# Fourier weight tiles read tile by tile, q swaps issued at the eviction, value products one score block later: a two-layer encoder on one core

## The chip, the cores and the metric

The kernel runs on one core of a Trainium2 chip. The metric is the device time of one execution in microseconds (us); lower is better. Before the change it took 2400.25 us, the median of three runs (2400.01 to 2401.22). All other times here are us too, from the span's start where they name a moment.

## The reference, cut to what matters

A trunk of two layers over 272 tokens (16 meta tokens and 256 others), 2048 channels, float32:

```python
h = rmsnorm(x)
q, k, v, f, ga, gf = split(h @ w_in)
q, k = rope_2d(rmsnorm(q)), rope_2d(rmsnorm(k))      # 8 query heads, 2 key heads, 128 wide
a = attention(q, k, v) @ w_attn_br                   # meta tokens, then two blocks of 128 queries
fr = real(fft2(f, axes=(tokens, 128 channels)))      # 8 channel groups
s = fr @ w_four
x = x + (sigmoid(ga) * a + sigmoid(gf) * s) @ w_out
h = rmsnorm(x)
x = x + (silu(conv3(h @ w_up_gate)) * (h @ w_up_val)) @ w_down
```

The output is x without the meta tokens.

## The kernel before

**Precision and weight tiles.** Every matrix product is made from float32 operands that are split into a high and a low part; three matmuls (high by high, high by low, low by high) stand for one. A weight tile is 128 partitions by 1024 (four blocks of 128 rows by 256 columns, 512 KB). Its way is: a DMA on SyncE's queue into a `raw` buffer (`load_raw`, L264; seven buffers), a cast on ScalarE to the high part `wh` (L300), a subtraction on VectorE to the low part `wl` (L303). `wh` and `wl` have three buffers each. The tiles come in one list in the order in which the matmul groups use them (`order`, then `chunks`).

**Groups.** `group` (L346) makes two output tiles of 128 rows in PSUM from several weight tiles. PSUM has eight tiles, four with the tag "mm" for these groups and four with the tag "aux" for everything else. A group that asks for a "mm" tile gets the one that was given out longest ago, and its first matmul into it waits until the last eviction from it is done.

**Fourier groups.** `four_group` (L388) multiplies the Fourier features by `w_four`, two weight tiles a group, eight groups a layer. By symmetry each output half m (0 and 1) takes two PSUM tiles, an even and an odd sum (`ps_s00`, `ps_s01` for m=0, `ps_s10`, `ps_s11` for m=1), and has 17 matmuls: 8 on the first weight tile, 8 on the second (L407 on `wh`, L408 on `wl`), and one with `w64` (L413). Then `s_evac` copies the second parts of both tiles out on ScalarE (L1206), adds the first parts on VectorE (L1207, `se` and `so`: these are the last reads of the two PSUM tiles) and multiplies the result with the gate. In layer 0 the two weight tiles of a Fourier group are folded first: VectorE makes sums and differences of two raw halves into `wpm` (L291, two instructions, one buffer), and `wh` and `wl` are made from that. In layer 1 they come folded from memory.

**What orders the work.** `advance` queues splits of coming weight tiles (`LOOK` = 2 tiles ahead) and starts loads; `pump` emits one queued split, or all up to a tile; `step` advances one of the generators in `shadow`, which emit the small work of normalisation, rotation and attention between the matmuls. This gives a program order; a scheduler then sets the order on each engine, and each engine runs its own in order. `tc.manual_schedule` (around q1 of layer 1) keeps the written order on the engines that it names.

**q and its rotation.** Each of four q groups a layer is evicted by `head_evac` (squares on ScalarE L910, the weighted copy `qp` on VectorE L911). `q_stage` then calls `swap` (L924): four DMAs on SyncE's queue that exchange blocks of 32 partitions of `qp` into `qs`. `rope` multiplies `qs` (L928) and `qp` (L929), adds them (L930), casts (ScalarE, L931) and subtracts (L933). In layer 1, between q1 and q2, stand the matmuls of `folded_f` (L843 on `wh`, L847 on `wl`).

**Attention.** `attention` goes over nine items of a key head: one for the meta tokens and eight (head h, query block i). For each: `scores` (three matmuls, maximum, exponential), `normalise` (L1086 writes `pn`), `transposed` (three transposes, L1095, into PSUM; ScalarE copies the high parts to `PH`, L1108, VectorE the low parts to `PL`, L1109), and after both blocks of a head `values` (L1118 to L1121: products of V with PH and PL).

Of the kernel before, what the change touches and what calls it, by code (L numbers as in the profile page):

```python
# [10 lines left out]
F32 = mybir.dt.float32  # L11
# [5 lines left out]
P = 128  # L17
# [16 lines left out]
MG = 2  # L34
# [43 lines left out]
TH = T // 2 + 2  # L78
# [79 lines left out]
def al(ap):  # L158
    if len(ap.shape) == 3:
        return ap.rearrange("p r (b a) -> p r a b", b=2)  # L160
    return ap.rearrange("p (b a) -> p a b", b=2)


def st2(ap):
    if len(ap.shape) == 3:
        return ap.rearrange("p r (a b) -> p r a b", b=2)
    return ap.rearrange("p (a b) -> p a b", b=2)
# [11 lines left out]
def encoder_kernel(ctx, tc, xT, params, consts, bmat, cfold, csign, w_fl, w_f64c, w_in, w_abr, w_four, w_f64, w_out, w_up, w_down, w_vn, w_dn, w_dt, out):  # L179
    nc = tc.nc  # L180
# [73 lines left out]
    raws, splits = {}, {}  # L254
    RAW, LOOK = 7, 2
# [13 lines left out]
    def advance(upto):  # L269
        while st["raw"] < min(upto + RAW + 2 * (upto > first_mix), len(chunks)):  # L270
            load_raw(st["raw"])
            st["raw"] += 1
        while st["fetch"] < min(upto, len(chunks)):
            i = st["fetch"]
            if i in folded:
                todo.append((i, lambda i=i: fold_w(i)))
            for a in (0, 2) if i <= 3 else (0,):
                todo.append((i, lambda i=i, a=a: split_w(i, a, a + 2 if i <= 3 else CW)))
            st["fetch"] += 1

    def pump(upto=None):
        if upto is None:
            if todo:
                todo.pop(0)[1]()
        while upto is not None and todo and todo[0][0] <= upto:
            todo.pop(0)[1]()
# [101 lines left out]
    def four_group(key, fr, x64, w64, evac):  # L388
        k, chs = order[st["grp"]]
        assert k == key, (k, key)  # L390
        st["grp"] += 1
        i0 = st["next"]
        st["next"] += len(chs)
        advance(i0 + 1 + LOOK)
        pump(i0 + 1)
        ws = [splits.pop(i0 + j) for j in range(2)]
        for m in range(MG):
            sl = slice(m * P, (m + 1) * P)
            ps = [psum.tile([P, 512], F32, tag="mm", name=f"ps_s{m}{e}") for e in range(2)]
            for j in range(2):  # L400
                h, lo = ws[j]
                for c in range(2):
                    kt = 2 * j + c
                    for e in range(2):
                        x = al(fr[:, kt, e])
                        o2 = st2(ps[e][:, :2 * TH].rearrange("p (r n) -> p r n", r=2))
                        nc.tensor.matmul(o2, h[:, 2 * e + c, sl], x, start=kt == 0, stop=False)  # L407
                        nc.tensor.matmul(st2(ps[e][:, :TH]), lo[:, 2 * e + c, sl], x[:, 0], start=False, stop=e == 1 and kt == 3)  # L408
                    step()
                    pump()  # L410
                if m == 1 and j == 0:
                    advance(i0 + 2 + LOOK)
            nc.tensor.matmul(st2(ps[0][:, :TH]), w64[:, sl], al(x64), start=False, stop=True)  # L413
            evac(m, ps)

    def first_groups(pss):
        assert order[st["grp"]][0] == (0, "f01")
# [191 lines left out]
    for l in range(DEPTH):  # L609
        last = l == DEPTH - 1  # L610
        lo = 14 if last else 0
# [4 lines left out]
        with tc.tile_pool(name=f"mix{l}", bufs=1) as mp:  # L616
# [285 lines left out]
            def head_evac(ps, gcol, name, lo):  # L902
                hp = rt(name)
                sq = rt(name + "s")
                if lo:
                    nc.gpsimd.memset(hp[:, :, 0:lo], 0.0)
                    nc.gpsimd.memset(sq[:, :, 0:lo], 0.0)
                for m in range(MG):
                    x = de(ps[m][:, :T - lo])
                    nc.scalar.activation(hv(sq[:, m, lo:T]), x, AF.Square)  # L910
                    nc.vector.scalar_tensor_tensor(hv(hp[:, m, lo:T]), x, gcol, hv(rstdB[:, lo:T]), op0=ALU.mult, op1=ALU.mult)  # L911
                return hp, sq
# [8 lines left out]
            def swap(hp):  # L921
                qs = rt("qs")
                for b in range(4):
                    tc.keep_in_program_order(nc.sync.dma_start(qs[32 * b:32 * b + 32, :, :], hp[32 * (b ^ 1):32 * (b ^ 1) + 32, :, :]))  # L924
                return qs
# [82 lines left out]
            for pn in pns:  # L1008
                nc.gpsimd.memset(pn[:, 0:P], 0.0)

            def q_stage(i, qp, qsq):
                kv, j = i // 2, i % 2
                sl = slice(2 * j, 2 * j + 2)
                if j == 0:
                    qvs.append(small.tile([P, 9], F32, tag="qv", name="qv"))
                    qsms.append(small.tile([P, 2, 4, NM], F32, tag="sqm", name="sqm", bufs=2))
                qv, qsm = qvs[kv], qsms[kv]
                qs = swap(qp)
                yield 3
                nc.vector.tensor_copy(qsm[:, :, 2 * j:2 * j + 2, :], qsq[:, :, 0:NM].unsqueeze(1).to_broadcast([P, 2, 2, NM]))  # L1020
                d4 = qv[:, 4 * j:4 * j + 4]
                sums_t(d4, [qsq[:, m, a:b] for m in range(MG) for a, b in BLK[1:]])
                d4 = d4.rearrange("p (m i) -> p m i", m=2)
                nc.vector.tensor_tensor(d4, d4, bc2(tok2[:, 1:3]), op=ALU.mult)
                if j:
                    yield 1
                    sums_t(qv[:, 8:9], [qsm.rearrange("p r h t -> p (r h t)")])
                    nc.vector.tensor_tensor(qv[:, 8:9], qv[:, 8:9], tok2[:, 0:1], op=ALU.mult)
                    nc.vector.tensor_scalar(qv, qv, 1.0 / HD, EPS, op0=ALU.mult, op1=ALU.add)
                    rq = small.tile([P, 9], F32, tag="rq", name="rq")  # L1030
                    pow_half(rq, qv)
                yield 6 - j
                yield from rope(qp, qs, qH[kv][:, sl, :], qL[kv][:, sl, :])
                if j:
                    rqs.append(rq)
                    if kv == 0:
                        push(attend(), 5)
# [9 lines left out]
            def attention(kv, rq):  # L1047
# [75 lines left out]
                    nc.vector.tensor_tensor(hv(qL[kv][:, h, lo:T]), de(po[:, :W]), hv(qH[kv][:, h, lo:T].bitcast(F32)), op=ALU.subtract)  # L1123

                items = [None] + [(h, i) for h in range(4) for i in range(2)]
                prev, ready, due = None, [], []
                for item in items + ["end", "end"]:
                    cur = None
                    if item != "end":
                        pe, sm = scores(item)  # L1130
                    yield 2
                    if item != "end":
                        cur = (item, normalise(pe, sm))
                    yield 1
                    if prev is not None:
                        transposed(*prev)
                        if prev[0] is not None and prev[0][1] == 1:
                            due.append(prev[0][0])
                        yield 1
                    if ready:  # L1140
                        values(ready.pop(0))
                    if prev is not None:
                        yield 1
                    ready, due = ready + due, []
                    prev = cur
                while ready:
                    values(ready.pop(0))
                    yield 1

            qH, qL = [], []  # L1150
            for i in range(4):
                if not (last and i == 1):
                    ps = group((l, "q", i), xr(lo), W)
                    qq = head_evac(ps, prm[:, P_QN + l:P_QN + l + 1], "qp", lo)
                if last:
                    if i in (0, 2):
                        until(hold, "vt" if i == 0 else "fold")
                        for t_, n in ((qH, "q1"), (qL, "q2")):
                            t_.append(mp.tile([P, 4, T], F32R, tag=n + "ab"[i // 2], name=n))
                elif i == 0:  # L1160
                    until(hold, "vt")
                    until(hold, "fold")
                    for t_, n in ((qH, "q1"), (qL, "q2")):
                        t = mp.tile([P, NH, T], F32R, tag=n, name=n)
                        t_ += [t[:, 0:4], t[:, 4:8]]
                if last and i == 1:
                    until(hold, "ahead")
                    with tc.manual_schedule(engines={mybir.EngineType.DVE}):
                        ps = group((l, "q", i), xr(lo), W)
                        with tc.manual_schedule(engines={mybir.EngineType.Activation}):  # L1170
                            qq = head_evac(ps, prm[:, P_QN + l:P_QN + l + 1], "qp", lo)
                            folded_f(slots, E)
                    o1_tiles()
                    push(folded_chan(E), 1)
                push(q_stage(i, *qq), 1)
# [395 lines left out]
```

## Time and profile before

| | |
|---|---|
| median of 3 runs | 2400.25 us |
| the profiled execution's own time | 2399.24 us |
| its span on the core | 2397.2 us |
| mean granted TensorE clock | 0.998 |
| TensorE busy | 2367.0 us (99%) |
| VectorE busy | 1819.8 us (76%) |
| ScalarE busy | 1307.1 us (55%) |

PE is TensorE (matmuls), PEld its weight loads, DVE VectorE, ACT ScalarE, SP or SPq SyncE and its DMA queue. L12 is line 12 of the kernel before; in the kernel after, lines behind `four_group` stand one to three higher. In the rows of a timeline the first two numbers are start and duration, and a bracket at the end gives the idle time of the engine before the instruction, and what ended it; "x2" joins instructions of one kind that follow each other. Rows of waits give the total, the number, and the longest. Rows of windows give the stretch and its length, then busy time (and instructions) of the engines asked for, the granted clock, the DMA share and GB/s. An engine's instructions overlap a little (a matmul of 0.28 starts 0.11 after the one before), so a row's place is read from starts.

### The profile page before, as it was taken

How to read it: one execution, taken by the hardware profiler on the slowest of the kernel's cores; microseconds unless marked ns; L12 is line 12 of the kernel's file. 1: busy time of each engine (PE TensorE's matmuls, PEld its weight loads, DVE VectorE, ACT ScalarE, POOL GpSimd, SP SyncE). 2: the span in 40 equal slices, each digit the busy share in tenths (PEclk: the TensorE clock that was granted, in tenths of full speed). 3: DMA queues.
4: the chain of work that ended last, by engine and by line, in shares of the span. 5: the costliest groups of instructions: out<-in, count | busy, mean ns of one | idle time of the engine just before them, and what ended most of it. 6: DMA issues, size and time to landing. Idle time of an engine off the chain costs nothing.

```text
span 2397.2 us, 47622 instructions
## 1 busy us (share of the span) xinstructions
PE 2367.0 (99%) x18992; PEld 2305.8 (96%) x18992; DVE 1819.8 (76%) x2889; ACT 1307.1 (55%) x1893; POOL 133.4 (6%) x265
## 2 busy tenths in 40 slices
PE   9999999999999999999999999999999999999999
PEld 8999999999999999999998999999989999999988
DVE  7787867877767556777568887776878889888798
ACT  6555534554444334444455555445676666666565
POOL 0000100100000000000000000000000000000000
PEclk9999999999999999999999999999999999999999
DMA  7556999989999999999875646888889988988887
GB/s 278 173 159 216 289 295 304 297 278 346 313 303 327 315 330 314 316 327 308 264 256 181 190 150 216 264 291 247 290 294 301 323 291 301 305 304 279 260 279 251
DMA packets 171215, 660.69 MB, mean 276 GB/s; under 512 B 19424, under 2 KB 24672, under 8 KB 170096
## 3 DMA queue, kind: packets, MB, share of 16 engines
q1 hardware_dynamic: 152528, 538.07, 64.0%
q0 software_dynamic: 17024, 117.45, 19.4%
q8 instruction: 149, 2.44, 0.4%
q10 hardware_dynamic: 1440, 2.13, 0.3%
q14 instruction: 74, 0.61, 0.1%
HBM read 635.91 MB, written 136.31 MB: 322 GB/s over the span
## 4 chain that ended last, share of the span: by engine, by line
PE 81%; DVE 6%; ACT 2%; DMA 1%; issue 1%; SPq 0%; POOL 0%; ACTq 0%; DVEq 0%; POOLq 0%
PE ps_p L1415 9%; PE ps_ug L374 6%; PE ps_ug L373 6%; PE ps_ug L372 6%; PE ps_uv L368 4%; PE ps_d L374 3%; PE ps_uv L373 3%; PE ps_uv L372 3%; PE ps_d L373 3%; PE ps_uv L374 3%; PE ps_d L372 3%; DVE wl L303 3%; PE ps_o L372 2%; PE ps_o L373 2%; PE ps_o L374 2%; PE ps_uv L369 2%
## 5 line engine op out<-in xcount | busy, mean ns | idle before, releaser
L303 DVE TENSOR_TENSOR wl<-raw,wh 128x1024 fp32r<-128x1024 f32 (+1 forms) x937 | 1127.6, 1217 | 469.8 <-ACT wh L300 458.4
L300 ACT CAST wh<-raw 128x1024 fp32r<-128x1024 f32 (+1 forms) x937 | 964.6, 1040 | 752.1 <-PE ps_ug L373 197.2
L374 PE MATMUL ps_ug<-xHL,wl 128*128 128x272 f32 (+1 forms) x1408 | 390.6, 277 | 0.8 <-DVE wl L303 0.6
L372 PE MATMUL ps_ug<-xHL,wh 128*128 128x272 f32 (+1 forms) x1408 | 390.7, 278 | 0.0
L373 PE MATMUL ps_ug<-xHL,wh 128*128 128x272 f32 (+1 forms) x1408 | 390.0, 277 | 0.0
L373 PEld LDWEIGHTS ps_ug<-xHL,wh 128*128 128x128 f32 x1408 | 267.4, 190 | 2.1
L372 PEld LDWEIGHTS ps_ug<-xHL,wh 128*128 128x128 f32 x1408 | 267.4, 190 | 2.1
L374 PEld LDWEIGHTS ps_ug<-xHL,wl 128*128 128x128 f32 x1408 | 267.5, 190 | 1.6 <-DVE wl L303 1.5
L372 PE MATMUL ps_uv<-xHL,wh 128*128 128x272 f32 x704 | 196.4, 279 | 0.0
L373 PE MATMUL ps_uv<-xHL,wh 128*128 128x272 f32 x704 | 196.4, 279 | 0.0
L374 PE MATMUL ps_uv<-xHL,wl 128*128 128x272 f32 x704 | 196.4, 279 | 0.0
L372 PE MATMUL ps_d<-gHL,wh 128*128 128x272 f32 x704 | 196.4, 279 | 0.0
L373 PE MATMUL ps_d<-gHL,wh 128*128 128x272 f32 x704 | 196.4, 279 | 0.0
L374 PE MATMUL ps_d<-gHL,wl 128*128 128x272 f32 x704 | 196.4, 279 | 0.0
L1415 PE MATMUL ps_p<-wh,opnd 128*128 128x512 f32 x688 | 177.5, 380 | 0.5 <-ACT wh L300 0.5
L368 PE MATMUL ps_uv<-xHL,wh 128*128 128x512 f32 x448 | 150.8, 383 | 0.1
L372 PE MATMUL ps_ga<-xHL,wh 128*128 128x272 f32 (+1 forms) x512 | 144.0, 281 | 0.0
L372 PE MATMUL ps_gf<-xHL,wh 128*128 128x272 f32 (+1 forms) x512 | 143.0, 279 | 0.0
L374 PE MATMUL ps_gf<-xHL,wl 128*128 128x272 f32 (+1 forms) x512 | 141.8, 277 | 0.0
L373 PE MATMUL ps_ga<-xHL,wh 128*128 128x272 f32 (+1 forms) x512 | 141.8, 277 | 0.0
L374 PE MATMUL ps_ga<-xHL,wl 128*128 128x272 f32 (+1 forms) x512 | 141.8, 277 | 0.0
L373 PE MATMUL ps_gf<-xHL,wh 128*128 128x272 f32 (+1 forms) x512 | 141.8, 277 | 0.0
(372 smaller groups left out, 5840.8 us busy)
## 6 DMA issues: line engine op xcount, KB each, us to landing
raw<-in_w_up SPq DMA_DIRECT2D x320, 512.0 KB, 5.6
raw<-in_w_in SPq DMA_DIRECT2D x191, 512.0 KB, 4.5
raw<-in_w_down SPq DMA_DIRECT2D x88, 512.0 KB, 6.8
raw<-ft SPq DMA_DIRECT2D x80, 512.0 KB, 4.8
raw<-in_w_out SPq DMA_DIRECT2D x64, 512.0 KB, 6.5
ft<-in_w_dn POOLq DMA_DIRECT2D x30, 1024.0 KB, 12.1
raw<-in_w_dn SPq DMA_DIRECT2D x60, 512.0 KB, 5.0
raw<-in_w_abr SPq DMA_DIRECT2D x32, 512.0 KB, 5.6
```

Of the source, the lines that this page charges most:

```text
L300: nc.scalar.copy(h[:, a:b], r[:, a:b])
L303: nc.vector.tensor_tensor(lo[:, a:b], r[:, a:b], h[:, a:b].bitcast(F32), op=ALU.subtract)
L368: nc.tensor.matmul(o2, h[:, c, sl], ab, start=kt == 0, stop=False)
L369: nc.tensor.matmul(o, lo[:, c, sl], ab[:, 0], start=False, stop=kt == nk - 1)
L372: nc.tensor.matmul(o, h[:, c, sl], a, start=kt == 0, stop=False)
L373: nc.tensor.matmul(o, h[:, c, sl], b, start=False, stop=False)
L374: nc.tensor.matmul(o, lo[:, c, sl], a, start=False, stop=kt == nk - 1)
L1415: nc.tensor.matmul(st2(ps[h]), x, al(w[:, 512 * h:512 * h + 512]), start=fresh and (s_, q) in BEGIN and first, stop=(s_, q) in END and end ...
```

## The change

There are three edits.

1. `four_group` asks for all four PSUM tiles at its start and goes over the weight tiles outside: first tile for m=0 and m=1, then second tile for m=0 and m=1, each m closed by its `w64` matmul and eviction. The second tile's split need only be emitted before its half, and `advance` for the third tile comes after the first half of the group rather than after the third quarter.
2. `swap(qp)` is called right after `head_evac` and not when `q_stage` begins.
3. A head's `values` becomes ready one item later (a list `soon` between `due` and `ready`).

```diff
-        pump(i0 + 1)
-        ws = [splits.pop(i0 + j) for j in range(2)]
-        for m in range(MG):
-            sl = slice(m * P, (m + 1) * P)
-            ps = [psum.tile([P, 512], F32, tag="mm", name=f"ps_s{m}{e}") for e in range(2)]
-            for j in range(2):
-                h, lo = ws[j]
+        pss = [[psum.tile([P, 512], F32, tag="mm", name=f"ps_s{m}{e}") for e in range(2)] for m in range(MG)]
+        for j in range(2):
+            pump(i0 + j)
+            h, lo = splits.pop(i0 + j)
+            for m in range(MG):
+                sl = slice(m * P, (m + 1) * P)
+                ps = pss[m]
                 for c in range(2):
...
-                if m == 1 and j == 0:
-                    advance(i0 + 2 + LOOK)
-            nc.tensor.matmul(st2(ps[0][:, :TH]), w64[:, sl], al(x64), start=False, stop=True)
-            evac(m, ps)
+                if j:
+                    nc.tensor.matmul(st2(ps[0][:, :TH]), w64[:, sl], al(x64), start=False, stop=True)
+                    evac(m, ps)
+            if j == 0:
+                advance(i0 + 2 + LOOK)
...
-                qs = swap(qp)
...
-                    ready, due = ready + due, []
+                    ready, soon, due = ready + soon, due, []
                     prev = cur
+                ready += soon
...
                     qq = head_evac(ps, prm[:, P_QN + l:P_QN + l + 1], "qp", lo)
+                    qq += (swap(qq[0]),)
```

TensorE in layer 0's second Fourier group, before: `wh72`, `wl72` are the first weight tile's parts, `wh73`, `wl73` the second's.

```order
L407 MATMUL ps_s01_3421<-fr_122,wh72_3358 128x276
L408 MATMUL ps_s01_3421<-fr_122,wl72_3359 128x138
L407 MATMUL ps_s00_3420<-fr_122,wh73_3394 128x276
L407 MATMUL ps_s01_3421<-fr_122,wh73_3394 128x276
L407 MATMUL ps_s10_3453<-fr_122,wh72_3358 128x276
L408 MATMUL ps_s00_3420<-fr_122,wl73_3395 128x138
```

The same place after:

```order
L407 MATMUL ps_s01_3421<-fr_122,wh72_3358 128x276
L408 MATMUL ps_s01_3421<-fr_122,wl72_3359 128x138
L407 MATMUL ps_s10_3422<-fr_122,wh72_3358 128x276
L408 MATMUL ps_s10_3422<-fr_122,wl72_3359 128x138
L407 MATMUL ps_s11_3423<-fr_122,wh72_3358 128x276
```

Before, the second tile was wanted from the group's ninth matmul on; after, from the seventeenth, with `ps_s10` and `ps_s11` written in between.

VectorE around the eviction of that group's m=0, before: `wl74` and `wl75` are the third and fourth tile counted from the group's first, 72.

```order
L303 TENSOR_TENSOR wl74_3427<-raw74_3177,wh74_3426 128x1024
L1229 TENSOR_TENSOR mL_3338<-th_2123,mH_3337 128x272
L1207 TENSOR_TENSOR se_3443<-ps_s00_3420,se_3443 128x138
L1207 TENSOR_TENSOR so_3444<-ps_s01_3421,so_3444 128x138
L1209 TENSOR_TENSOR sp_3449<-se_3443,so_3444 128x138
L1210 TENSOR_TENSOR sp_3449<-se_3443,so_3444 128x134
L1212 SCALAR_TENSOR_TENSOR th_3127<-th_3127,sp_3449 128x272
L303 TENSOR_TENSOR wl75_3470<-raw75_3209,wh75_3469 128x1024
```

The same place after (L1210 is the add that was L1207):

```order
L303 TENSOR_TENSOR wl74_3429<-raw74_3158,wh74_3428 128x1024
L1232 TENSOR_TENSOR mL_3338<-th_2123,mH_3337 128x272
L303 TENSOR_TENSOR wl75_3451<-raw75_3209,wh75_3450 128x1024
L1210 TENSOR_TENSOR so_3460<-ps_s01_3421,so_3460 128x138
L1210 TENSOR_TENSOR se_3459<-ps_s00_3420,se_3459 128x138
L1212 TENSOR_TENSOR sp_3465<-se_3459,so_3460 128x138
```

The split of `wl75` (the group's first tile plus three) has moved from behind the eviction to directly ahead of its adds; on ScalarE `wh75` stands ahead of the copies in the same way. All sixteen groups show this.

SyncE's queue at layer 1's q0, before: `raw451` to `raw454` are weight loads, `qs` the swap.

```order
L264 DMA raw451_16310<-fw_66 128x1024
L264 DMA raw452_16350<-fw_66 128x1024
L264 DMA raw453_16399<-fw_66 128x1024
L924 DMA qs_16409<-qp_16385 32x2x272 x4
L264 DMA raw454_16444<-fw_66 128x1024
```

The same place after:

```order
L264 DMA raw451_16310<-fw_66 128x1024
L264 DMA raw452_16350<-fw_66 128x1024
L925 DMA qs_16393<-qp_16385 32x2x272 x4
L264 DMA raw453_16404<-fw_66 128x1024
L264 DMA raw454_16444<-fw_66 128x1024
```

The swap stands one weight load earlier.

More of the change, by code (lines that the diff above doesn't have):

```diff
@@ L1009, in encoder_kernel, with q_stage @@
                 nc.gpsimd.memset(pn[:, 0:P], 0.0)
-            def q_stage(i, qp, qsq):
+            def q_stage(i, qp, qsq, qs):
                 kv, j = i // 2, i % 2
@@ L1125, in attention @@
                 items = [None] + [(h, i) for h in range(4) for i in range(2)]
-                prev, ready, due = None, [], []
+                prev, ready, due, soon = None, [], [], []
                 for item in items + ["end", "end"]:
@@ L1171, in encoder_kernel @@
                             qq = head_evac(ps, prm[:, P_QN + l:P_QN + l + 1], "qp", lo)
+                            qq += (swap(qq[0]),)
                             folded_f(slots, E)
```

## The prediction

> **What bounds the kernel now.** I read the page first, then the waits of TensorE, then single stretches on the timeline, the chain of waits, and a table of the sixteen Fourier groups.
>
> ```profile
> PE 2367.0 (99%) x18992; PEld 2305.8 (96%) x18992; DVE 1819.8 (76%) x2889; ACT 1307.1 (55%) x1893; POOL 133.4 (6%) x265
> ```
>
> TensorE is busy 99% of the span. The change issues the same matmuls, so time can come only from TensorE's idle time, and new idle time is a loss one for one. The waits of TensorE (us in total, times, longest) name what there is to win:
>
> ```profile
> PE ps_s L408 <- DVE wl L303: 4.3, 8, 0.7
> PE ps_f L847 <- DVE wl L303: 3.9, 1, 3.9
> PE ps_pt L1095 <- DVE pn L1086: 2.9, 4, 1.3
> PE ps_pv L1119 <- DVE PL L1109: 2.2, 4, 1.2
> PE ps_pv L1118 <- ACT PH L1108: 2.0, 5, 0.5
> PE ps_s L407 <- ACT wh L300: 2.0, 5, 1.1
> ```
>
> L407/L408 are Fourier groups waiting for a weight tile (6.3), L847 is one late tile beside the q swap (3.9), L1118/L1119 the value products (4.2). Each edit aims at one of these.
>
> **Part 1, Fourier groups.** The table of windows has each group from its first matmul to the next group's first; shown are one of layer 0's first half, one of its second, layer 1's second and last, and the sum of all sixteen.
>
> ```profile
> 245.47:250.71 5.24, 4.34 (x37) 1.00 0.91 222
> 388.83:393.31 4.48, 4.12 (x36) 1.00 0.65 164
> 1473.53:1477.38 3.85, 3.85 (x36) 1.00 0.79 214
> 1668.48:1672.34 3.86, 3.86 (x36) 1.00 0.90 150
> sum 73.47, PE 66.58; mean PE 4.16
> ```
>
> Free of waits a group takes 3.86 (its 34 matmuls, two per 0.23). Layer 1's groups have nothing to win; the idle time over all sixteen, 73.47 - 66.58 = 6.9, is nearly all layer 0's.
>
> The edit spends eight matmuls (0.92) more on the first tile, so the second may come 0.9 later. But it moves two things against itself. First, half m=0 ends after three quarters of the group instead of half, 1.0 later, and the next group's first matmuls write into m=0's two PSUM tiles and wait for their VectorE adds (L1207). Second, the order of after puts the split of the weight tile three on from the group's first (wh on ScalarE, wl on VectorE; call it tile 3) ahead of those adds, where before had it behind. Layer 1, on VectorE and then ScalarE:
>
> ```profile
> 1474.79 1.22 DVE L303 TENSOR_TENSOR wl<-raw,wh 128x1024 fp32r<-128x1024 f32 x1
> 1475.92 0.76 DVE L1229 TENSOR_TENSOR mL<-th,mH 128x258 fp32r<-128x258 f32 x2
> 1476.60 0.29 DVE L1207 TENSOR_TENSOR so<-ps_s,so 128x138 f32<-128x138 f32 x1
> 1475.52 0.28 ACT L1206 COPY so<-ps_s 128x138 f32<-128x138 f32 x1 [0.19 <-PE ps_s L408]
> 1476.53 2.00 ACT L300 CAST wh<-raw 128x1024 fp32r<-128x1024 f32 x2 [0.56 <-ACT se L1206]
> ```
>
> Here the first add ends at 1476.89 and the next group starts at 1477.38: 0.49 to spare. After: tile 3 needs the buffer of the group's first tile (three buffers), which the eighth pair of matmuls leaves 1.94 after the start (8 x 0.23 and the last one's end), at 1475.47. Then wh 1.05 (half of 2.00, with its start) ends at 1476.55, wl at 1.22 ends at 1477.80, and the add 0.3 later, 1478.10: 0.72 behind 1477.38. The same chain from the group's own start holds in the other six of layer 1: 7 x 0.72 = 5.0. The first one there carries score and value work among its matmuls; I take 0.5. Layer 1: +5.5.
>
> Layer 0, first half (group at 245.47), VectorE, then the group's largest wait on TensorE:
>
> ```profile
> 246.75 1.23 DVE L303 TENSOR_TENSOR wl<-wpm,wh 128x1024 fp32r<-128x1024 f32 x1
> 248.59 1.22 DVE L303 TENSOR_TENSOR wl<-raw,wh 128x1024 fp32r<-128x1024 f32 x1
> 249.73 0.43 DVE L1229 TENSOR_TENSOR mL<-th,mH 128x272 fp32r<-128x272 f32 x1
> 250.29 0.29 DVE L1207 TENSOR_TENSOR so<-ps_s,so 128x138 f32<-128x138 f32 x1
> 248.03 0.44 PE L408 MATMUL ps_s<-fr,wl 128*128 128x138 f32 x2 [0.64 <-DVE wl L303]
> ```
>
> The second tile's low part ends at 247.98 either way; with the new order the matmuls that need it stand at 247.5, so about 0.9 of the group's 1.4 (5.24 - 3.86) goes. Nothing of it reaches the end, since VectorE works without a break from 246.75: the 1.14 of tile 3's split (start to next start) enters ahead of the adds, the second of which then ends at 250.58 + 1.14 = 251.7, the first at 251.5. The next group starts at 251.55 instead of 250.71: +0.85, three times (2.55). In the group before these, two matmuls also wait for the gate's evictions, +0.6; the first of the second half is covered, -0.1. For the last three (group at 388.83), VectorE:
>
> ```profile
> 390.26 0.43 DVE L1184 TENSOR_TENSOR th<-ps_gf,rstdB 128x272 f32<-128x272 f32 x1
> 391.76 0.30 DVE L1207 TENSOR_TENSOR so<-ps_s,so 128x138 f32<-128x138 f32 x1
> ```
>
> The fourth PSUM tile is now wanted at 389.98 but is the gate's until 390.69; the first tile's matmuls end 0.69 later at 391.4, wh at 392.45, wl at 393.6, add at 393.95 against a start at 393.31: +0.65 each, 1.95. Layer 0: 0.6 + 2.55 - 0.1 + 1.95 = +5.0. **Part 1 is +10.5.** Bounds: -6.9, if nothing waits for the adds and all tile waits go; +13, if each add also waits for ScalarE's copy behind wh (16 x 0.28 = 4.5, over half of the groups). I take +10.5, since it is put together from durations that all stand above; the likely spread is +7 to +13.
>
> The Trainium skill, "Perfetto Trace Analysis", section "Optimizing Tensor Performance", wants independent matmul groups to rotate through PSUM banks so that one's evacuation overlaps the next one's matmuls. Filling all four tiles to the end works against that; layer 1 of before, with two tiles at a time and no idle, agrees, and no run here shows the other side yet.
>
> **Part 2, the q swaps.** The chain of waits around the one late tile (start, duration):
>
> ```profile
> 1284.41 0.40 DVE qp L911
> 1286.64 0.32 SPq L264
> 1287.05 0.60 SPq L924
> 1288.98 3.83 DMA qs<-qp
> 1292.93 0.73 DVE qs L928
> 1296.45 1.23 DVE wl L303
> 1297.73 0.48 PE ps_f L847
> ```
>
> q0's eviction (L911) is done by 1284.8, but the swap's four DMAs stand on SyncE behind a weight load that waits until 1286.58 for a buffer. VectorE waits at L928 for the swap, and the low part that TensorE needs is queued behind q's rotation:
>
> ```profile
> 1288.03 2.36 DVE L303 TENSOR_TENSOR wl<-raw,wh 128x1024 fp32r<-128x1024 f32 x2
> 1292.93 0.73 DVE L928 TENSOR_TENSOR qs<-qs,cst 128x544 f32<-128x544 f32 x1 [2.54 <-DMA qs<-qp]
> ```
>
> The DMA issues in this stretch, with the us to landing at the end:
>
> ```profile
> qs<-kp SPq DMA_DIRECT2D x4, 68.0 KB, 2.4
> qs<-qp SPq DMA_DIRECT2D x4, 68.0 KB, 3.8
> ```
>
> After, only SyncE's order changes here: the swap goes ahead of that load, issues from 1284.9 to 1287.4, and lands by about 1289.8 to 1291.2 (2.4 to 3.8 after the last issue). VectorE is at work until 1290.39, so L928 starts 2.54 sooner at best and 1.7 at worst, and the low part is there at about 1295.2; TensorE's wait falls from 3.9 to about 1.4. The load passed starts 0.8 later and is not wanted for several tiles (seven raw buffers). The clock, in windows (us, TensorE busy, granted clock):
>
> ```profile
> 1293.90:1296.80 2.90, 0.00 (x0) 0.00 (x0) 2.21 (x5) 1.59 (x2) 0.00 (x0) 0.99 0.29 113
> 1296.80:1303.60 6.80, 5.87 (x27) 5.79 (x28) 4.04 (x6) 1.99 (x2) 0.00 (x0) 0.50 0.45 154
> 1303.60:1310.00 6.40, 6.40 (x59) 6.33 (x59) 6.33 (x9) 4.08 (x6) 0.00 (x0) 1.00 0.59 186
> ```
>
> 2.9 after TensorE went idle the clock fell to half for 6.8 us. The 27 matmuls there took 5.87; at the next window's 6.40/59 = 0.108 they take 2.93, so half speed cost 2.9. An idle of 1.4 ends before the point where it fell. **Part 2 is -2.5 - 2.9 = -5.4**; bounds 0 (swap lands no sooner) and -6.8 (the whole wait goes). The Trainium skill, "TensorE: Matmul & The Clock Gate", section "Part 1: The HAM clock gate", has a free-running window of 3413 ns, one of which idle halves the clock. The 6.8 us at half speed are two such, so the trace agrees; by the page too, an idle of 1.4 cannot hold a window.
>
> The other layer-1 swap that moves passes two small constant loads and later weight loads, the one in layer 0 two loads; VectorE does not wait for either in before. I cost both at nothing; 0.3 each if a weight load came late.
>
> **Part 3, value products a block later.** The largest wait is in layer 1:
>
> ```profile
> 1384.42 0.38 PE L1118 MATMUL ps_pv<-PH,VH 128*128 128x258 f32 x1 [0.51 <-ACT PH L1108]
> 1387.11 0.38 PE L1119 MATMUL ps_pv<-PL,VH 128*128 128x258 f32 x1 [1.18 <-DVE PL L1109]
> ```
>
> In layer 1 the probability tile's second half reads, by range, the block that was transposed last, whichever that is; a block later the one before it is safe, but a new one has been transposed just ahead again. So I let the outlier 1.18 shrink to 0.5 (-0.7), and two of the other seven go, at (4.2 - 0.51 - 1.18)/7 = 0.36 each (-0.7): **-1.4**. Bounds: -4.2 (all waits on PH and PL go) and +1.5 (the score blocks' own waits at L1095, 2.9, grow by half).
>
> **Sum.** 10.5 - 5.4 - 1.4 = +3.7. The profiled execution took 2399.24 (span 2397.2), 1.0 under the median of 2400.25; so the forecast is 2399.24 + 3.7 + 1.0 = **2403.9**. A measurement of this kernel can tell about 0.2% (4.8 us) from no change: "same" is 2395.45 to 2405.05.
>
> **The rivals.**
> - *The forecast*, chance 0.54, own range 2400 to 2408 (part 1 by +7 to +13): 0.02 faster, 0.42 same, 0.10 slower.
> - *The adds don't bind.* If the next group's first matmuls found their tiles free, the tile waits would go for nothing: -6.9 - 5.4 - 1.4 = -13.7, 2386.5. For: 4.48 and 5.24 stand beside 3.86. Against: the 0.49 of slack in layer 1 is smaller than the 1.0 by which m=0 ends later, even without tile 3's split. 0.14, faster.
> - *The swap gains nothing and the clock still falls* (slower). It decides if the swap lands after 1292.3: the DMA rows would need 5 us from the last issue, where 3.8 was the slowest; or if TensorE's idle still covers 1293.8 to 1296.8. Then 10.5 - 1.4 = +9.1, 2409.3. 0.18, slower.
> - *The value waits move rather than go*: with +1.5 for part 3 the sum is +6.6, 2406.8. For it: in the rows above the product waits for a block just transposed, and the order keeps such a block ahead of it. 0.14: 0.10 slower, 0.04 same.
>
> Together: faster 0.16, same 0.46, slower 0.38. The range 2395 to 2409.5 leaves out the second case and a little above the third.
>
> **What would show it.** Right: layer 1's Fourier windows at 4.5 to 4.6 with waits of matmuls L372 on L1210's adds (so/se), sixteen in all; L408 waits down to a few tenths; L847's wait near 1.4 and no window at clock 0.50. Wrong: Fourier windows at 3.86 in layer 1 (then the second case), an L847 wait over 3 (third), or waits at L1118/L1119 still above 4 in sum.

## The result, and the profile after

The changed kernel takes 2405.36 us, the median of 19 runs (2403.27 to 2407.84); the kernel before, measured beside it, 2400.36 (19 runs). The ratio is 1.0019, 95% interval [1.0012, 1.0027]: about 5 us slower (3 to 6.5 by the interval), right at the edge of the 0.2% that the prediction counts as no change. The forecast was 2403.9, with a range of 2395 to 2409.5. The profiled execution has a span of 2403.6, against 2397.2, so the two traces lie 6.4 apart.

The waits of TensorE in the kernel after (us in total, times, longest) answer to those of before:

```profile
PE ps_gf L372 <- DVE so L1210: 5.0, 5, 1.5
PE ps_a L372 <- DVE so L1210: 4.1, 8, 0.6
PE ps_ga L372 <- DVE so L1210: 2.0, 2, 1.5
PE ps_s L407 <- DVE th L1187: 1.9, 3, 0.7
PE ps_s L408 <- DVE wl L303: 1.5, 5, 0.6
PE ps_f L848 <- DVE wl L303: 1.4, 2, 1.3
PE ps_pt L1095 <- DVE pn L1086: 3.4, 5, 0.9
PE ps_pv L1119 <- DVE PL L1109: 2.1, 2, 1.1
PE ps_pv L1118 <- ACT PH L1108: 1.4, 3, 0.7
```

The first three rows are new: the groups that follow a Fourier group (gf, a, ga) wait at their first matmul for the adds `so` that evict m=0, fifteen times, 11.1 us. The sixteenth, behind layer 1's first Fourier group, does not wait for them: that group is held up inside, by a value product.

```profile
1455.29 0.38 PE L1119 MATMUL ps_pv<-PL,VH 128*128 128x258 f32 x1 [1.12 <-DVE PL L1109]
```

The fourth row is new too: `ps_s11` waits for a gate's eviction. The waits of Fourier groups for weight tiles fell from 6.3 to 1.5 (the prediction had a few tenths), the late tile's (now L848) from 3.9 to 1.3 at the longest. The value products' fell from 4.2 to 3.5, and the score blocks' (L1095) rose from 2.9 to 3.4.

The Fourier groups in windows (stretch, length, TensorE busy, clock, DMA share, GB/s), the four places shown of before, and the sum of all sixteen:

```profile
244.08:250.27 6.19, 4.50 (x36) 1.00 0.83 195
390.25:395.66 5.41, 4.23 (x36) 1.00 0.59 151
1473.16:1477.72 4.56, 4.02 (x36) 1.00 0.67 167
1672.64:1677.25 4.61, 4.03 (x37) 1.00 0.93 168
sum 84.45, PE 68.72; mean PE 4.29
```

The sum went from 73.47 to 84.45: +11.0, where the prediction had +10.5. The busy column rose by 2 as well (its ends are modelled); the number of matmuls is the same, so the length is what counts.

VectorE in layer 1's second Fourier group, then ScalarE there, after:

```profile
1476.23 1.22 DVE L303 TENSOR_TENSOR wl<-raw,wh 128x1024 fp32r<-128x1024 f32 x1
1477.37 0.30 DVE L1210 TENSOR_TENSOR so<-ps_s,so 128x138 f32<-128x138 f32 x1
1475.13 1.05 ACT L300 CAST wh<-raw 128x1024 fp32r<-128x1024 f32 x1 [0.18 <-ACT mH L1231]
1476.09 0.27 ACT L1209 COPY so<-ps_s 128x138 f32<-128x138 f32 x1
```

The group starts at 1473.16. Tile 3's cast starts 1.97 later (forecast 1.94), its low part ends at 1477.45, the add at 1477.67, and the next group starts at 1477.72. The copy was out at 1476.36, so for the 1.0 between it and the add's start the PSUM tile waits for nothing but VectorE's turn.

The late tile, and the clock behind it, after. First TensorE's row, then the windows:

```profile
1299.50 0.33 PE L848 MATMUL ps_f<-hA,wl 128*128 128x138 f32 x1 [1.26 <-DVE wl L303]
```

```profile
1298.20:1299.50 1.30, 0.04 (x2) 1.00 0.10 41
1299.50:1303.00 3.50, 3.50 (x30) 1.00 0.64 189
```

In the chain of waits there the swap now issues at 1289.27, right after the eviction, and is no wait of VectorE's any more; the clock stays at 1.00. How much that brought is read from two waits of TensorE that stand on either side in both kernels, before and then after:

```profile
1283.05 0.44 PE L918 MATMUL ps_ss<-cst,qps 128*128 128x128 f32 x2 [0.78 <-ACT qps L910]
1369.90 0.52 PE L1095 MATMUL ps_pt<-cst,pn 128*128 128x128 f32 x3 [0.62 <-DVE pn L1086]
```

```profile
1287.45 0.44 PE L919 MATMUL ps_ss<-cst,qps 128*128 128x128 f32 x2 [0.78 <-ACT qps L911]
1369.33 0.52 PE L1095 MATMUL ps_pt<-cst,pn 128*128 128x128 f32 x3 [0.60 <-DVE pn L1086]
```

The same work takes 86.85 before and 81.88 after: -4.97. The stretch between these two waits is 81.88 or 81.89 in the traces of all six kernels with the swap edit (the runs below included), and 86.48 to 86.85 in the four without it.

### The profile page after: what moved, and what is told of

It reads as the page before. It is cut to its first block, busy times and chain, and to the rows that moved or that the text cites. A ratio compares the mean times of both kernels' runs of the same rounds, so it can differ in the third digit from the quotient of the medians.

```text
span 2403.6 us, 47628 instructions
## 1 busy us (share of the span) xinstructions
PE 2366.8 (98%) x18992; PEld 2304.5 (96%) x18992; DVE 1818.9 (76%) x2889; ACT 1306.7 (54%) x1893; POOL 130.8 (5%) x265
## 4 chain that ended last, share of the span: by engine, by line
PE 85%; DVE 8%; ACT 3%; DMA 2%; issue 2%; POOL 0%; SPq 0%; DVEq 0%; ACTq 0%; POOLq 0%
PE ps_p L1418 9%; PE ps_ug L374 6%; PE ps_ug L373 6%; PE ps_ug L372 6%; DVE wl L303 4%; PE ps_uv L368 3%; PE ps_d L372 3%; PE ps_uv L374 3%; PE ps_uv L373 3%; PE ps_d L374 3%; PE ps_uv L372 3%; PE ps_d L373 3%; PE ps_o L374 2%; PE ps_o L373 2%; PE ps_o L372 2%; ACT wh L300 2%
## 5 line engine op out<-in xcount | busy, mean ns | idle before, releaser
L374 PE MATMUL ps_ug<-xHL,wl 128*128 128x272 f32 (+1 forms) x1408 | 391.0, 278 | 2.4 <-DVE wl L303 2.3
L374 PEld LDWEIGHTS ps_ug<-xHL,wl 128*128 128x128 f32 x1408 | 267.5, 190 | 3.8 <-DVE wl L303 3.5
L374 PE MATMUL ps_uv<-xHL,wl 128*128 128x272 f32 x704 | 196.4, 279 | 0.0
L374 PE MATMUL ps_d<-gHL,wl 128*128 128x272 f32 x704 | 196.4, 279 | 0.0
L372 PE MATMUL ps_gf<-xHL,wh 128*128 128x272 f32 (+1 forms) x512 | 143.3, 280 | 5.0 <-DVE so L1210 5.0
L374 PE MATMUL ps_gf<-xHL,wl 128*128 128x272 f32 (+1 forms) x512 | 141.8, 277 | 0.0
L374 PE MATMUL ps_ga<-xHL,wl 128*128 128x272 f32 (+1 forms) x512 | 141.8, 277 | 0.0
L372 PE MATMUL ps_o<-mH,wh 128*128 128x272 f32 (+1 forms) x512 | 141.8, 277 | 0.0
```

The costliest lines, as they stand in the source:

```text
L372: nc.tensor.matmul(o, h[:, c, sl], a, start=kt == 0, stop=False)
L374: nc.tensor.matmul(o, lo[:, c, sl], a, start=False, stop=kt == nk - 1)
```

## The experiments

The theory (A) is the prediction's: the Fourier loop loses some 11 us because the next group waits for the eviction of m=0's PSUM tiles; the swap wins about 5; the value products about 1. The rivals: the edits disturb each other (B), the early split on a busy VectorE costs by itself rather than through the PSUM tiles (B of the second series), m=0's later end alone makes the wait (C).

All runs are compared with the kernel before on the same chip: the first four rows on one, where it took 2400.55, the last four on another, where it took 2400.27.

| kernel | us | ratio to before, 95% interval | sixteen Fourier windows |
|---|---|---|---|
| Fourier loop alone | 2413.61 | 1.0056 [1.0042, 1.0070] | 85.2 |
| swap alone | 2396.81 | 0.9985 [0.9974, 0.9995] | |
| value products alone | 2399.82 | 0.9996 [0.9987, 1.0004] | |
| swap and values | 2395.41 | 0.9983 [0.9974, 0.9992] | 74.3 |
| after, eviction kept first | 2391.73 | 0.9971 [0.9959, 0.9982] | 71.0 |
| after, m=1 in other PSUM tiles | 2389.61 | 0.9958 [0.9946, 0.9971] | 68.3 |
| the same, values late in layer 0 only | 2388.96 | 0.9961 [0.9948, 0.9975] | 67.8 |
| Fourier loop alone, m=1 in other PSUM tiles | 2395.95 | 0.9981 [0.9972, 0.9991] | 68.1 |

**One edit at a time.** The Fourier loop alone is the new `four_group` in the kernel before.

> Only the Fourier loop (edit 1) on the kernel before. Theory A (the next group waits for the adds that evict m=0): +11 us, about 2411, the sixteen Fourier windows sum to about 84.5 as in the kernel after; the late low part at L847 and the half clock are still there. Rival B (the three edits interact, and the loss in after comes from the swap or value edits shifting the tiles): under +5, 2401 to 2405, windows under 80.

It measured +13 (interval +10 to +17), windows of 85.2: theory A for the place and the size, B is out. Here all sixteen groups are followed by a wait for the adds. The 2 beyond the expected +11 are within the interval; a half-speed stretch in the profiled execution (last section) is one possible cause.

The swap alone is the moved call:

```diff
-                qs = swap(qp)
+                    qq += (swap(qq[0]),)
```

> Only the q swap (edit 2) on the kernel before. Theory A: -5 us, about 2395: the wait at the late tile falls from 3.9 to about 1.3 (-2.6) and no window at clock 0.50 follows (-2.3 to -2.9). Rival B (the clock falls whatever the wait): -2.6, about 2397.7, with a window at clock 0.50.

-3.7 (interval -6 to -1). The time does not tell -5 from -2.6. In the trace the late tile waits 1.26 and no stretch after it shows a clock under 1.00:

```profile
1295.00 0.33 PE L847 MATMUL ps_f<-hA,wl 128*128 128x138 f32 x1 [1.26 <-DVE wl L303]
```

That is theory A for the profiled execution, which was the fastest of the eleven (2392.96). It is one of three with a mean clock of 1.000; the other eight show 0.998 or 0.999 and average 4 us more, so their clock fell somewhere; where, no trace shows.

The value products alone:

```diff
-                    ready, due = ready + due, []
+                    ready, soon, due = ready + soon, due, []
```

> Only the value products (edit 3) on the kernel before. Theory A from the trace of after: -1.5 in layer 0, +0.3 in layer 1, together -1.2, about 2399. Rival B (the waits only move): 0 +- 0.5, 2400.3. The half clock after the late tile stays in both.

-0.7, interval -3 to +1: not told from nothing. The waits of TensorE in its trace, to be read against those of before:

```profile
PE ps_f L847 <- DVE wl L303: 4.1, 1, 4.1
PE ps_pt L1095 <- DVE pn L1086: 3.4, 5, 0.8
PE ps_pv L1119 <- DVE PL L1109: 2.0, 2, 1.1
PE ps_pv L1118 <- ACT PH L1108: 1.7, 4, 0.7
```

Scores and values together wait 7.1 in both kernels (2.9 + 2.2 + 2.0, and 3.4 + 2.0 + 1.7). Of the Fourier groups, layer 0's first is 0.57 shorter than before (5.50 against 6.07) and layer 1's first 1.08 longer (7.18 against 6.10). This edit moves waits; rival B holds as well as A.

Both without the Fourier loop:

> Edits 2 and 3 without the Fourier loop. Theory A (terms add): -5.0 - 1.2 = -6.2, about 2394.2, Fourier windows at 73.5 as before. Rival B (interaction): over 2397.

-5 (interval -6 to -2): this fits terms that add, though the interval also holds rival B's 2397. The Fourier windows are back at 74.3; layer 1's first takes 7.47 of it, with a half-speed stretch that the last section shows.

**Which part of the Fourier loop loses.** Here the kernel after keeps its four PSUM tiles, but the adds stand ahead of tile 3's split:

```diff
-            nc.scalar.copy(h[:, a:b], r[:, a:b])
+            keep(i, nc.scalar.copy(h[:, a:b], r[:, a:b]))
...
+        kept.add(i0 + 3)
...
                     evac(m, ps)
-            if j == 0:
-                advance(i0 + 2 + LOOK)
+                    if m == 0:
+                        advance(i0 + 2 + LOOK)
```

`keep` holds the split of that tile in program order, on ScalarE and VectorE; the eviction's copies and adds are held in the same way. Tile 3 is also queued later, behind m=0's eviction, so the run changes the order by two means at once.

> The kernel after with its four PSUM tiles, but with the eviction of m=0 kept ahead of tile 3's split on VectorE and ScalarE (kept in program order, and the queueing of tile 3 after m=0's eviction). Theory A: m=0's copies and adds then end about 3.6 after the group's start, before 3.86, so layer 1's windows fall back to 3.86 to 3.95 and layer 0's to 4.4 to 5.0; sum 70 to 74, 2392 to 2395. Rival C (m=0's later end alone makes the wait): layer 1's windows stay at 4.4 or more, 2402 or more.

The windows of layer 1's last seven groups are back at 3.86 and layer 0's at 4.6 to 5.1; the sum is 71.0, 13.4 less than after, and the time 2391.73. Of the 13.4, 1.1 is layer 1's first group (6.62 to 5.50), where the value product no longer waits. Three of the sixteen and their sum, and VectorE in layer 1's second group:

```profile
242.54:247.51 4.97, 4.50 (x36) 1.00 0.93 226
384.56:389.28 4.72, 4.07 (x37) 1.00 0.54 138
1464.35:1468.20 3.85, 3.85 (x36) 1.00 0.79 198
sum 71.03, PE 66.73; mean PE 4.17
```

```profile
1466.75 0.76 DVE L1239 TENSOR_TENSOR mL<-th,mH 128x258 fp32r<-128x258 f32 x2
1467.68 0.30 DVE L1217 TENSOR_TENSOR se<-ps_s,se 128x138 f32<-128x138 f32 x1 [0.17 <-ACT se L1216]
1467.90 0.29 DVE L1217 TENSOR_TENSOR so<-ps_s,so 128x138 f32<-128x138 f32 x1
```

The first add ends at 1467.98, 3.63 after the start, ahead of 3.86: m=0's later end alone makes no wait in layer 1, rival C is out. In layer 0 adds that come late still cost 0.7 in three waits. The split in front of the adds was needed for the loss in layer 1; whether it would be enough with m=0 ending as early as before was not run.

Now the order of after, with tile 3's split ahead of the adds, but m=1 in the other four PSUM tiles:

```diff
-        pss = [[psum.tile([P, 512], F32, tag="mm", name=f"ps_s{m}{e}") for e in range(2)] for m in range(MG)]
+        pss = [[psum.tile([P, 512], F32, tag=("mm", "aux")[m], name=f"ps_s{m}{e}") for e in range(2)] for m in range(MG)]
```

> The kernel after, with m=1's two PSUM tiles taken from the other four (tag aux), so that the next group's first tiles are not those of m=0; the order on VectorE and ScalarE keeps tile 3's split ahead of the adds in all sixteen groups. Theory A (the loss is the wait of the next group for PSUM tiles): the waits for the adds go, windows sum to 65 to 67 (16 x 3.86, the score work in one, and 2 to 3 of tile waits), 2405.4 - 18 = about 2387. Rival B (tile 3's early split on the busy VectorE is itself what costs): windows stay over 76, 2397 or more.

Windows and VectorE of that kernel:

```profile
241.66:246.23 4.57, 4.13 (x37) 1.00 0.94 231
382.30:386.16 3.86, 3.86 (x37) 1.00 0.49 145
1460.81:1464.66 3.85, 3.85 (x36) 1.00 0.70 190
sum 68.33, PE 64.72; mean PE 4.04
```

```profile
1463.88 1.22 DVE L303 TENSOR_TENSOR wl<-raw,wh 128x1024 fp32r<-128x1024 f32 x1
1465.02 0.30 DVE L1210 TENSOR_TENSOR so<-ps_s,so 128x138 f32<-128x138 f32 x1
```

The add still comes late, at 1465.02, 0.36 after the next group has started at 1464.66; nobody waits for it. So tile 3's split in front costs nothing by itself, and the loss of the Fourier loop is the wait for PSUM tiles: 84.5 goes to 68.3, a little above the expected 65 to 67. Layer 1's first group stays at 6.61 (6.62 in the kernel after): what it lost there was not a wait for PSUM tiles. The waits for weight tiles that the loop was to shorten are then a gain of 5 against the 73.5 of before (2.5 of them are left, all in layer 0). The time, 2389.61, is 2.6 above what was expected, 0.4% under the kernel before and 0.7% under the kernel after.

> Only the Fourier loop on the kernel before, with m=1 in the other four PSUM tiles. Theory A: the tile waits that the loop was to remove are then gained, windows at 65 to 67 against 73.5, -7 us, about 2393; the 3.9 wait and the half clock at the late tile stay. Rival B: no gain over before, 2400 or more.

That loop on the kernel before measured -4.3 (interval -7 to -2) with windows at 68.1: theory A, a little less than the expected -7.

> As the run with m=1 in the other PSUM tiles, but the value products a block later in layer 0 alone. Theory A (edit 3 wins 1.5 in layer 0 and loses about 0.5 in layer 1, and its 1.1 wait beside the first Fourier group of layer 1 can bring the half clock): 0.5 to 2 faster than that run. Rival (edit 3 is worth the same in both layers): the same or slower than it.

0.65 faster than with values late in both layers, less than the intervals can tell. In the trace the first Fourier group of layer 1, where the last value products lie, takes 6.10 with values not late there and 6.61 in the run before:

```profile
1438.29:1444.39 6.10, 5.50 (x47) 1.00 0.42 128
```

```profile
1437.28:1443.89 6.61, 5.49 (x49) 1.00 0.43 137
```

So 0.5 of the value edit's gain in layer 0 is lost here by the trace; that it shows in the time is open.

## Why the prediction was right, point by point

- **The sum** was +3.7, measured +5.0, and the signs of its two large terms were right. The likeliest case came about: the adds do bind, the swap does land in time. The third rival, value waits that move rather than go, is not excluded.
- **Part 1**, +10.5 against +11.0. Layer 1: seven groups at 0.72 each, measured 0.65 to 0.75. Layer 0's second to fourth: 0.85, measured 0.95, 0.94, 0.90. The first of the second half: -0.1, measured -0.2. Two terms were mis-sized. The last three had +0.65 and took +0.93, +0.99, +0.92: `ps_s11` got the gate's PSUM tile when the working said, 1.9 after the group's start, but tile 3's cast then started 2.84 after it (393.09 in the group at 390.25), where the working had 2.57 (391.4 - 388.83); it had put nothing between that release and the next matmul, and too little for the last matmul's end. The first group had +0.6 and took +0.1; beside the run of swap and values, where that group takes 5.50, the loop costs 0.66 there.
- **Luck in part 1.** Layer 1's first group had +0.5 and took +0.52, but not by waiting for the adds: the value product's wait of 1.12 held it up, which belongs to part 3. The misses in layer 0, -0.5 in one group and +0.9 over three, partly cancel. So the total of part 1 is nearer than its terms.
- **An argument that failed**: the later end alone was to bind in layer 1, 0.49 of slack against 1.0. With the eviction first it did not (3.63 against 3.86). The 0.49 was not m=0's own slack: before, the copy was out at 1475.80 and the add stood behind `mL` on VectorE until 1476.60. That tile 3's split in front and the shared PSUM tiles carry the loss in layer 1 is shown by the runs with the eviction first and with other PSUM tiles.
- **All four PSUM tiles held.** Of the Trainium skill's "Perfetto Trace Analysis", section "Optimizing Tensor Performance", the advice to rotate groups through PSUM banks now has its other side: all four tiles held cost 84.5 - 68.3 = 16 with tile 3's split ahead of the eviction. With the eviction first the sum is 71.0, 2.7 above 68.3.
- **Part 2**, -5.4 against -4.97 in the trace. The wait fell to 1.26 (forecast 1.4), the work of L928 (L929 after) started with no wait for the swap, and no half clock followed.
- **Part 3**, -1.4, is the weak term. By itself the edit measured -0.7, not told from nothing, and the waits at L1118 and L1119 sum to 3.5 after, between the 2.8 forecast and the 4 that was to speak for the rival. Before layer 0's first Fourier group the waits on PH and PL (0.7) are gone; in layer 1 they sum to 3.4 both before and after. The outlier shrank only from 1.18 to 0.93, and a new wait of 1.12 came in the first Fourier group.
- **Not in the sum**: after layer 1's Fourier groups both kernels do the same work, yet the profiled execution of after loses another 1.5 there; its waits of `ps_ug` at L374 for low parts are 2.3, against 0.6. Waits there of 0.8 or 0.9 stand in every experiment's trace but that of the swap alone (longest 0.4), so they are not the work of one edit; what brings them was not tried.
- **A step of the argument that failed**, though the place came out right: that an idle of 1.4 is too short for the clock to fall. The last section has the rows.

## What to carry to other kernels

When a loop is turned so that one input comes later, ask what is held longer for it: here the price was paid not by the group that holds the PSUM tiles but by the next one, and it shows in the profile as that group's first matmul waiting for an eviction. Freeing a buffer earlier lets a scheduler put a long prefetch in front of a short eviction; look at the order on the evicting engine before trusting the slack seen in the old trace. Where a gain and a loss of like size meet, measure the edits apart: the same three edits with m=1's output in the other four PSUM tiles are 0.4% faster than the kernel before instead of 0.2% slower.

## What the runs showed of the hardware that was not expected

The clock fell to half without a long idle. In the run of the Fourier loop alone, TensorE had waited 1.47 for the adds; windows there:

```profile
249.70:253.10 3.40, 1.93 (x17) 1.00 1.06 267
253.10:256.50 3.40, 3.40 (x16) 0.51 1.04 294
256.50:259.90 3.40, 3.40 (x31) 0.99 1.42 598
```

And in the run of swap and values, after waits of 0.36 and 1.07:

```profile
1446.20:1449.60 3.40, 2.12 (x18) 1.00 0.49 154
1449.60:1453.00 3.40, 3.25 (x15) 0.54 0.68 184
1453.10:1456.50 3.40, 3.40 (x31) 0.97 0.38 141
```

Stretches that were 57% and 62% busy (1.93 and 2.12 of 3.40) were each followed by 3.4 at half speed, 16 and 15 matmuls in place of 31, about 1.7 lost. The Trainium skill, "TensorE: Matmul & The Clock Gate", section "Part 1: The HAM clock gate", has in its table the half clock after at least one idle window of about 3.4; the length of 3.4 agrees, the idle does not, and here the measurement decides. The kernel after has three waits of 1.4 to 1.5 and no such stretch in its profiled execution, so equal waits fall on either side. The long wait at the late tile brought half speed in all four profiled kernels that have it (3.9 to 4.3: before, the Fourier loop alone in both versions, values alone); the six with 1.25 or 1.26 there kept full speed.
